# A state space mixer whose output projection runs three groups behind instead of two, with the last group's steps placed between its shares

## The chip, the cores and the metric

The kernel runs on one core of a Trainium2 chip. The metric is the device time of one launch in microseconds; the runs shown are medians over repeated launches. TensorE (PE) is granted one of two clock levels, 2.4 GHz (shown as 1.00) or 1.2 GHz (0.50).

## The reference

A decoder trunk of two layers on 256 tokens of width 1024, in float32. Each layer is a half SwiGLU block, a token mixer, and another half SwiGLU block. The first layer's mixer is a Mamba-2 state space mixer with 8 groups of 4 heads of 64 channels and a state of 128; the second's is latent attention. The change touches the first mixer only, which is:

```
def mamba2_mixer(h, w_in, conv_w, conv_b, dt_bias, a_log, d_skip, norm_w, w_out):
    proj = h @ w_in
    z, xbc, dt = ...                       # 2048, 2048 + 2*1024, 32 columns
    xbc = silu(causal_depthwise_conv(xbc, conv_w, conv_b))
    xs, bm, cm = ...                       # 8 groups x 4 heads x 64; 8 x 128; 8 x 128
    y = ssd_chunked(xs, dt, a, bm, cm)     # chunks of 128 tokens
    y = y + d_skip * xs
    g = (y * silu(z)) in 8 groups of 256
    g = g * rsqrt(mean(g*g, within the group) + EPS) * norm_w
    return g @ w_out                       # 2048 -> 1024
```

## The kernel before, in words

**Matrix products.** Every float32 product is made of three matmuls on rounded parts (`mm3`, L203 to L205): high weight by high activation, high weight by low activation, low weight by high activation. A weight tile arrives by DMA on SP's queue (`raw`, four buffers, 128x1024, which is 8 matrices of 128x128 and so 24 matmuls of the mixer). ACT casts it to the high part (`whi`, L119), DVE subtracts to get the low part (`wlo`, L121); five pairs of `whi`/`wlo` can be held. The tiles come in one fixed order, that in which the host packed them (`packed_weights`), and `ws.next()` hands them out in the same order, so a step that is moved takes its weights with it.

**The mixer.** For each group g of 8 there are these steps:

- `stage_x`: 16 `mm3` (48 matmuls) into an accumulator, then a convolution: DVE scales into `up` (L383), ACT makes two products, POOL adds them (L398), DVE adds two more taps for two tiles (L401), ACT applies SiLU.
- `stage_z`: 48 matmuls, scaled on DVE (L645), SiLU on ACT.
- `stage_bc(g + 2)`: 48 matmuls and a convolution for B and C, two groups ahead.
- `stage_a`, for two groups at once in every even g: C by B on PE (L509, L510), copied by ACT to `cbm`; a DMA from SP brings `acb` (L516, two buffers); DVE adds masks (L522, L525), ACT takes exponentials (L531, L534) and DVE multiplies into `dec` (L538).
- `stage_t`: four transposes of xs (L552), scaled by DVE to `xd` (L557).
- `stage_y`: eight matmuls of `dec` by `xd` (L571, L574), DVE adds the skip term (L581, `y`), POOL multiplies by z (L586, `gt`) and squares and adds (L239, L242, L243, `gsq`).
- `stage_n`: a sum over the channels on PE (L249), DVE scales it (L253, `rsv`), POOL takes the power -1/2 (L257, `rsc`).
- `stage_o`: PE spreads `rsc` (L264), DVE multiplies (L601, `gn`), ACT and DVE split the result into `yh` (L228) and `yl` (L229).
- `stage_out(g)`, the share of the group in the output: 48 matmuls, six into each half of four accumulators that are kept until the mixer's end, when x is added (L626).

PSUM has four `acc` and four `misc` buffers. Projections use `acc` until the first share takes all four for the output, from then on `misc`. Every engine runs its instructions in one fixed order. That order is made by a scheduler when the program is built: it starts from the order in which the code is written, and moves instructions past one another within the limits of buffers and data.

Of the kernel before, what the change touches and what calls it, by code (L numbers as in the profile page):

```python
# [10 lines left out]
F32 = mybir.dt.float32  # L11
# [8 lines left out]
P = 128  # L20
# [3 lines left out]
KD = D // P  # L24
# [5 lines left out]
NG = 8  # L30
# [134 lines left out]
def trunk(ctx: ExitStack, tc: tile.TileContext, xt, pos, wts, small, consts, out):  # L165
# [201 lines left out]
    def ssm(n, nxt):  # L367
        with tc.tile_pool(name="mp", bufs=2) as mp:
# [134 lines left out]
            def stage_a(g):  # L503

                bc = st.pop((g, "bc"))
                ps = misc_ps()
                nc.tensor.matmul(ps[:, :T], bc[:, 0, :P], bc[:, 1], start=True, stop=True)  # L509
                nc.tensor.matmul(  # L510
                    ps[:, T : T + P], bc[:, 0, P:], bc[:, 1, P:], start=True, stop=True
                )
                cb = mp.tile([P, 3 * P], F32, tag="cbm", name="cbm")
                nc.scalar.copy(cb, ps[:, : 3 * P])
                acb = mp.tile([P, 4, T], F32, tag="acb", name="acb")
                nc.sync.dma_start(  # L516
                    acb, acd[4 * g : 4 * g + 4].unsqueeze(0).broadcast_to([P, 4, T])
                )

                mask = cst[:, C_TM : C_TM + P].unsqueeze(1).broadcast_to([P, 4, P])  # L520
                acm = mp.tile([P, 4, P], F32, tag="acm", name="acm")
                nc.vector.tensor_tensor(  # L522
                    out=acb[:, :, :P], in0=acb[:, :, :P], in1=mask, op=ALU.add
                )
                nc.vector.tensor_tensor(out=acm, in0=acb[:, :, P:], in1=mask, op=ALU.add)  # L525
                ms = []
                for hp in range(2):
                    dec = mp.tile([P, 2, 3 * P], F32, tag="dec", name="dec", bufs=8)
                    for j in range(2):
                        h = 4 * g + 2 * hp + j  # L530
                        in_turn(nc.scalar.activation(  # L531
                            dec[:, j, :T], acb[:, 2 * hp + j], AF.Exp, bias=bias[:, h : h + 1]
                        ))
                        in_turn(nc.scalar.activation(  # L534
                            dec[:, j, T:], acm[:, 2 * hp + j], AF.Exp,
                            bias=bias[:, NH + h : NH + h + 1],
                        ))
                    nc.vector.tensor_tensor(  # L538
                        out=dec, in0=dec,
                        in1=cb.unsqueeze(1).broadcast_to([P, 2, 3 * P]),  # L540
                        op=ALU.mult,
                    )
                    ms.append(dec)
                st[g, "m"] = ms

            def stage_t(g):

                xs = st[g, "x"]
                ps = misc_ps()
                for b in range(NB):  # L550
                    for j in range(2):
                        nc.tensor.transpose(  # L552
                            ps[:, (2 * b + j) * P : (2 * b + j + 1) * P],
                            xs[:, j, b * P : (b + 1) * P], ident,
                        )
                xd = mp.tile([P, NB, 4, HD], F32, tag="xd", name="xd")
                nc.vector.tensor_tensor(  # L557
                    out=xd, in0=ps.rearrange("p (b h c) -> p b h c", b=NB, h=4),
                    in1=dt.rearrange("p (b h) -> p b h", b=NB)[:, :, 4 * g : 4 * g + 4]
                    .unsqueeze(3).broadcast_to([P, NB, 4, HD]),  # L560
                    op=ALU.mult,
                )
                st[g, "xd"] = xd
# [28 lines left out]
            def stage_n(g):  # L592
                st[g, "r"] = rs_col(st.pop((g, "q")), 2 * P)
# [13 lines left out]
                two_part(yh, yl, gn)  # L607
                st[g, "y"] = yh, yl

            def stage_out(g, half):  # L610

                yh, yl = st[g, "y"]
                if not outs:
                    outs.extend(acc_ps() for _ in range(KD // 2))
                for d in range(4 * half, 4 * half + 4):
                    o = outs[d // 2][:, d % 2 * T : (d % 2 + 1) * T]
                    for k in range(2):

                        mm3(
                            o, ws.next(), yh[:, k], yl[:, k],  # L620
                            g == 0 and d % 2 == 0 and k == 0,
                            g == NG - 1 and d % 2 == 1 and k == 1,
                        )
                    if g == NG - 1 and d % 2 == 1:
                        both = x[:, d - 1 : d + 1]
                        nc.vector.tensor_tensor(  # L626
                            out=both, in0=both, in1=wide(outs[d // 2]), op=ALU.add
                        )
                        use_x(nxt, d - 1)
                        use_x(nxt, d)  # L630
# [21 lines left out]
            for g in range(NG):  # L652
                stage_x(g)
                if g == 0:
                    bias, acd = sums()
                else:
                    stage_y(g - 1)
                stage_z(g)
                if g:
                    stage_n(g - 1)  # L660
                stage_t(g)
                if g % 2 == 0:
                    stage_a(g)
                    stage_a(g + 1)
                if g:
                    stage_o(g - 1)
                if g + 2 < NG:
                    stage_bc(g + 2)
                if g == last:
                    stage_y(last)  # L670
                if g > 1:
                    stage_out(g - 2, 0)
                    stage_out(g - 2, 1)
            stage_n(last)
            stage_out(last - 1, 0)
            stage_o(last)
            stage_out(last - 1, 1)
            stage_out(last, 0)
            stage_out(last, 1)

    def angles():

# [369 lines left out]
def packed_weights(a):  # L1052

    seq = []

    def add(ts):
        seq.append(np.ascontiguousarray(ts.reshape(-1, P, P)))

    def ffn(i, j):
        g, u = tiles_of(a["ffn_w_gate"][i, j]), tiles_of(a["ffn_w_up"][i, j])  # L1060
        gu = np.stack([g, u])
        add(gu[:, :, :2].transpose(1, 2, 0, 3, 4))
        add(gu[:, :, 2:].transpose(2, 1, 0, 3, 4))
        add(tiles_of(a["ffn_w_down"][i, j]).transpose(1, 0, 2, 3))

    def by_column(w):
        add(tiles_of(w).transpose(1, 0, 2, 3))

    def by_pair(w0, w1):
        add(np.stack([tiles_of(w0)[:, 0], tiles_of(w1)[:, 0]], 1))  # L1070

    def narrow(w):

        w = w.reshape(KD, P, NARROW).transpose(1, 0, 2).reshape(P, KD * NARROW)
        add(w.reshape(P, -1, P).transpose(1, 0, 2))

    ffn(0, 0)
    w = a["ssm_w_in"][0]
    wz, wx, wb, wc, wd = np.split(w, [DI, 2 * DI, 2 * DI + 1024, 2 * DI + 2048], axis=1)
    narrow(wd)  # L1080

    def bc(g):
        by_column(wb[:, P * g : P * g + P])
        by_column(wc[:, P * g : P * g + P])

    def out(g):
        by_column(a["ssm_w_out"][0][256 * g : 256 * g + 256])

    bc(0)
    bc(1)  # L1090
    for g in range(NG):
        by_column(wx[:, 256 * g : 256 * g + 256])
        by_column(wz[:, 256 * g : 256 * g + 256])
        if g + 2 < NG:
            bc(g + 2)
        if g > 1:
            out(g - 2)
    out(NG - 2)
    out(NG - 1)
    ffn(0, 1)  # L1100
    ffn(1, 0)
    w = a["mla_w_in"][0]
    wq, wkv, wr = np.split(w, [QL, QL + KVL], axis=1)
    by_pair(wq[:, :P], wq[:, P : 2 * P])
    by_column(wq[:, 2 * P :])
    by_column(wkv)
    narrow(wr)
    kv = a["mla_w_kv_b"][0].reshape(KVL, MH, NOPE + VD)
    wk, wv = (
        tiles_of(np.ascontiguousarray(part).reshape(KVL, MH * 64))  # L1110
        for part in (kv[:, :, :NOPE], kv[:, :, NOPE:])
    )
    wq = tiles_of(a["mla_w_q_b"][0])
    for i in range(2):
        for t, n, c in ((wq, 3, 2 * i), (wq, 3, 2 * i + 1), (wk, 4, i), (wv, 4, i)):
            add(t[:, n * c : n * c + n])
    by_column(a["mla_w_out"][0][:512])
    by_column(a["mla_w_out"][0][512:])
    ffn(1, 1)

    tiles = np.concatenate(seq)
    out = np.empty(tiles.size, tiles.dtype)
    n0 = 0
    for n in SIZES:
        out[n0 * P * P : (n0 + n) * P * P] = (
            tiles[n0 : n0 + n].transpose(1, 0, 2).reshape(-1)
        )
        n0 += n
    assert n0 == len(tiles)
    return out  # L1130
# [63 lines left out]
```

## Time and profile before

| | |
|---|---|
| median of the runs | 1134.09 us (1133.56 to 1136.16, 3 runs) |
| the profiled execution | 1136.57 us, its span 1134.5 us |
| mean granted clock | 0.982 |
| PE busy | 1092.2 us (96% of the span) |
| DVE busy | 852.1 us (75%) |
| ACT busy | 642.8 us (57%) |
| POOL busy | 211.5 us (19%) |

The span is the part of the profiled execution between its first and last instruction. An engine's share is its busy time over the span; a PE at half clock counts as busy too.

### The profile page before, as it was taken

The page shows a single profiled execution, that of the slowest core. Times are in us where ns is not written, and L with a number is a line of the kernel's source. Part 1 is how long each engine was busy: PE and PEld are TensorE (multiplying, and loading weights), DVE is VectorE, ACT ScalarE, POOL GpSimd, SP SyncE. Part 2 cuts the span into 40 slices and gives each one's busy share as a digit, 9 for nine tenths or more (in the row PEclk, how much of TensorE's full clock was granted, in tenths as well). Part 3 has the DMA queues.
Part 4 walks back from the last instruction along what each step waited for, and adds up shares of the span by engine and source line. Part 5 has one row for each costly group of instructions (what it writes and reads, how often), then busy time and mean ns, then how long its engine had stood idle before and what let it go on. Part 6 is the DMA issues. An engine that isn't in the chain of part 4 may idle for free.

```text
span 1134.5 us, 18325 instructions
## 1 busy us (share of the span) xinstructions
PE 1092.2 (96%) x6902; PEld 974.0 (86%) x6902; DVE 852.1 (75%) x1370; ACT 642.8 (57%) x1102; POOL 211.5 (19%) x201
## 2 busy tenths in 40 slices
PE   7999999998999988999999999999996999999998
PEld 6888888997998987888888988888995689888887
DVE  7877776789777876877777687776779768877653
ACT  5655544677657564555554475554465545655541
POOL 7000012204223224200002200001247025000000
PEclk9999999998989998999999999999998999999999
DMA  7766665565345442655555575555543025665661
GB/s 240 226 185 187 187 187 171 181 201 175 133 146 168 158 133 97 200 187 189 189 186 168 186 236 191 185 186 187 168 148 117 1 64 170 204 186 186 187 204 55
DMA packets 55320, 191.58 MB, mean 169 GB/s; under 512 B 6304, under 2 KB 8384, under 8 KB 55232
## 3 DMA queue, kind: packets, MB, share of 16 engines
q1 hardware_dynamic: 55200, 190.41, 52.5%
q8 instruction: 54, 0.88, 0.3%
q14 instruction: 34, 0.28, 0.1%
q0 software_dynamic: 32, 0.00, 0.0%
HBM read 189.31 MB, written 1.08 MB: 168 GB/s over the span
## 4 chain that ended last, share of the span: by engine, by line
PE 80%; DVE 11%; DMA 3%; ACT 2%; issue 2%; POOL 2%; SPq 0%; DVEq 0%; ACTq 0%
PE acc L214 40%; PE misc L214 21%; PE acc L203 3%; PE acc L204 3%; PE acc L205 3%; DVE wlo L121 3%; PE misc L203 2%; DVE ca L401 2%; PE misc L204 2%; PE misc L205 2%; DMA acb<-acd 1%; PE acc L983 1%; POOL xsq L243 1%; DMA cst<-consts 1%; DVE qc L892 1%
## 5 line engine op out<-in xcount | busy, mean ns | idle before, releaser
L121 DVE TENSOR_TENSOR wlo<-raw,whi 128x1024 fp32r<-128x1024 f32 (+3 forms) x345 | 433.6, 1260 | 158.4 <-ACT whi L119 157.3
L119 ACT CAST whi<-raw 128x1024 fp32r<-128x1024 f32 (+3 forms) x355 | 364.8, 1031 | 251.9 <-PE acc L214 139.6
L214 PE MATMUL misc<-xp,whi 128*128 128x512 f32 x704 | 279.8, 401 | 0.4 <-ACT whi L119 0.4
L214 PE MATMUL acc<-xp,whi 128*128 128x512 f32 x704 | 274.8, 393 | 0.0
L214 PE MATMUL acc<-ap,whi 128*128 128x512 f32 x616 | 215.5, 397 | 0.0
L214 PE MATMUL misc<-xp,wlo 128*128 128x256 f32 x704 | 196.5, 281 | 3.5 <-DVE wlo L121 3.5
L214 PE MATMUL acc<-xp,wlo 128*128 128x256 f32 x704 | 197.1, 282 | 0.2 <-DVE wlo L121 0.2
L214 PE MATMUL acc<-ap,wlo 128*128 128x256 f32 x616 | 167.8, 281 | 0.0
L214 PEld LDWEIGHTS acc<-xp,whi 128*128 128x128 f32 x704 | 132.2, 188 | 33.1
L214 PEld LDWEIGHTS misc<-xp,whi 128*128 128x128 f32 x704 | 132.4, 189 | 23.2 <-ACT whi L119 0.7
L214 PEld LDWEIGHTS misc<-xp,wlo 128*128 128x128 f32 x704 | 132.7, 189 | 11.4 <-DVE wlo L121 4.2
L214 PEld LDWEIGHTS acc<-ap,whi 128*128 128x128 f32 x616 | 113.9, 188 | 25.5
L214 PEld LDWEIGHTS acc<-xp,wlo 128*128 128x128 f32 x704 | 133.0, 189 | 1.3 <-DVE wlo L121 0.5
L214 PEld LDWEIGHTS acc<-ap,wlo 128*128 128x128 f32 x616 | 115.4, 188 | 2.8
L320 ACT COPY g<-misc 128x256 f32<-128x256 f32 x88 | 32.7, 371 | 82.2 <-PE misc L214 82.0
L239 POOL TENSOR_TENSOR xsq<-x 128x256 f32<-128x256 f32 x6 | 3.7, 612 | 366.0 <-DVE x L364 351.5
L242 POOL TENSOR_TENSOR sq<-x 128x256 f32<-128x256 f32 x42 | 40.2, 963 | 115.3 <-DVE x L364 112.2
L205 PE MATMUL acc<-xp,wlo 128*128 128x256 f32 x216 | 61.6, 285 | 0.0
L204 PE MATMUL acc<-xp,whi 128*128 128x256 f32 x216 | 61.6, 285 | 0.0
L203 PE MATMUL acc<-xp,whi 128*128 128x256 f32 x216 | 61.4, 286 | 0.0
L203 PE MATMUL misc<-xp,whi 128*128 128x256 f32 x208 | 60.6, 291 | 0.0
L204 PE MATMUL misc<-xp,whi 128*128 128x256 f32 x208 | 59.5, 286 | 0.0
(249 smaller groups left out, 1926.4 us busy)
## 6 DMA issues: line engine op xcount, KB each, us to landing
raw<-wts SPq DMA_DIRECT2D x341, 512.0 KB, 4.0
acb<-acd SPq DMA_DIRECT2D x8, 512.0 KB, 3.7
raw<-wts SPq DMA_DIRECT2D x8, 256.0 KB, 2.8
raw<-wts SPq DMA_DIRECT2D x4, 384.0 KB, 3.0
out<-x SPq DMA_DIRECT2D x8, 128.0 KB, 3.3
x<-xt SPq DMA_DIRECT2D x3, 256.0 KB, 7.1
raw<-wts SPq DMA_DIRECT2D x4, 192.0 KB, 2.3
sm<-small SPq DMA_DIRECT2D x1, 283.5 KB, 7.9
```

Of the source, the lines that this page charges most:

```text
L119: self.nc.scalar.copy(hi[:, :n], raw[:, :n])
L121: eng.tensor_tensor(out=lo[:, :n], in0=raw[:, :n], in1=hi[:, :n].bitcast(F32), op=ALU.subtract)
L203: nc.tensor.matmul(o, w[0], h, start=start, stop=False)
L204: nc.tensor.matmul(o, w[0], l, start=False, stop=False)
L205: nc.tensor.matmul(o, w[1], h, start=False, stop=stop)
L214: nc.tensor.matmul(dst, a, b, start=start and i == 0, stop=stop and i == 1)
L242: nc.gpsimd.tensor_tensor(out=sq, in0=src, in1=src, op=ALU.mult)
L243: nc.gpsimd.tensor_tensor(out=acc, in0=acc, in1=sq, op=ALU.add)
L320: nc.scalar.copy(t, ps[:, T:])
L401: nc.vector.scalar_tensor_tensor(out=a[:, j], in0=up[:, j, k : k + T], scalar=w(t, k), in1=a[:, j], op0=ALU.mult, op1=ALU.add,)
L892: eng.tensor_tensor(out=a, in0=a, in1=r[:, b, o].unsqueeze(2).broadcast_to(list(a.shape)), op=ALU.mult,)
L983: nc.tensor.matmul(o, vt[:, 0, c], pT[:, :T], start=True, stop=False)
```

## The change

The share of a group in the output comes three groups behind the projections instead of two, and the host packs the output's tiles in that order. Within an iteration the steps of earlier groups change their places: `stage_o` comes right behind `stage_x` and for the group before last, `stage_y` behind `stage_z`, `stage_n` behind `stage_bc`, `stage_t` behind all of these. After the loop, the last group's transposes, products and norm are written between the last three shares, which are cut by output columns. `dec` has six buffers instead of eight.

```diff
-                    dec = mp.tile([P, 2, 3 * P], F32, tag="dec", name="dec", bufs=8)
+                    dec = mp.tile([P, 2, 3 * P], F32, tag="dec", name="dec", bufs=6)
...
-            def stage_out(g, half):
+            def stage_out(g, d0=0, d1=KD):
...
-                for d in range(4 * half, 4 * half + 4):
+                for d in range(d0, d1):
...
                 stage_x(g)
                 if g == 0:
                     bias, acd = sums()
-                else:
-                    stage_y(g - 1)
+                if g > 1:
+                    stage_o(g - 2)
                 stage_z(g)
                 if g:
-                    stage_n(g - 1)
-                stage_t(g)
+                    stage_y(g - 1)
                 if g % 2 == 0:
                     stage_a(g)
                     stage_a(g + 1)
-                if g:
-                    stage_o(g - 1)
                 if g + 2 < NG:
                     stage_bc(g + 2)
-                if g == last:
-                    stage_y(last)
-                if g > 1:
-                    stage_out(g - 2, 0)
-                    stage_out(g - 2, 1)
+                if g:
+                    stage_n(g - 1)
+                if g < last:
+                    stage_t(g)
+                if g > 2:
+                    stage_out(g - 3)
+
+            stage_t(last)
+            stage_o(last - 1)
+            stage_out(last - 2, 0, 4)
+            stage_y(last)
+            stage_out(last - 2, 4, 8)
+            stage_out(last - 1, 0, 4)
             stage_n(last)
-            stage_out(last - 1, 0)
+            stage_out(last - 1, 4, 6)
             stage_o(last)
-            stage_out(last - 1, 1)
-            stage_out(last, 0)
-            stage_out(last, 1)
+            stage_out(last - 1, 6, 8)
+            stage_out(last)
...
-        if g > 1:
-            out(g - 2)
-    out(NG - 2)
-    out(NG - 1)
+        if g > 2:
+            out(g - 3)
+    for g in range(NG - 3, NG):
+        out(g)
```

The scheduler settles what this does to each engine. **PE at the first share, before:** the spread of group 0 (L264), the products of group 1, and then at once the first matmuls of group 0's share (`yh_2737`, `yl_2738`), which take the accumulators `acc_3118` to `acc_3121`.

```order
L264 MATMUL misc_2731<-cst_73,rsc_2722 128x128 x2
L571 MATMUL misc_2891<-dec_2471,xd_2729 64x256
L574 MATMUL misc_2891<-dec_2471,xd_2729 64x128
...
L571 MATMUL misc_2891<-dec_2477,xd_2729 64x256
L574 MATMUL misc_2891<-dec_2477,xd_2729 64x128
L203 MATMUL acc_3118<-yh_2737,whi_2943 128x256
L203 MATMUL acc_3119<-yh_2737,whi_2943 128x256
...
L204 MATMUL acc_3118<-yl_2738,whi_2943 128x256
L205 MATMUL acc_3118<-yh_2737,wlo_2944 128x256
```

**The same place after:** behind the spread (`rsc_2797`) and group 1's products come four matmuls of `stage_a` and a projection (`xp` is the mixer's input).

```order
L264 MATMUL misc_2881<-cst_73,rsc_2797 128x128 x2
L571 MATMUL misc_2956<-dec_2464,xd_2804 64x256
...
L574 MATMUL misc_2956<-dec_2470,xd_2804 64x128
L509 MATMUL misc_2975<-bc_2537 128x256
L510 MATMUL misc_2975<-bc_2537 128x128
L509 MATMUL misc_2997<-bc_2778 128x256
L510 MATMUL misc_2997<-bc_2778 128x128
L203 MATMUL acc_3108<-xp_75,whi_2924 128x256
```

The first share (`yh_2887`) now starts 164 matmuls later in PE's order than before and fills its accumulators one after the other (`acc_3366` to `acc_3369`). Before its last accumulator stands the norm's sum of group 2:

```order
L205 MATMUL acc_3368<-yh_2887,wlo_3281 128x256
L249 MATMUL misc_3352<-ones_76,gsq_3272 128x1 x2
L203 MATMUL acc_3369<-yh_2887,whi_3280 128x256
L204 MATMUL acc_3369<-yl_2888,whi_3280 128x256
```

**DVE in the stretch ahead of the first shares, before:** the scaling of group 1's norm (`rsv_2978`) stands behind one mask pair and ahead of the `dec` of groups 2 and 3.

```order
L522 TENSOR_TENSOR acb_3678<-acb_3678,cst_73 128x4x128
L525 TENSOR_TENSOR acm_3680<-acb_3678,cst_73 128x512
L253 TENSOR_SCALAR rsv_2978<-misc_2975 128x2
L557 TENSOR_TENSOR xd_2987<-misc_2982,dt_2199 128x512
L121 TENSOR_TENSOR wlo_3186<-raw_3152,whi_3185 128x1024
L538 TENSOR_TENSOR dec_2999<-dec_2999,cbm_2992 128x768
```

**After:** group 1's scaling (`rsv_3097`) stands behind three of the four `dec` of groups 2 and 3 and the mask pair `acb_3604`. Later on DVE, from the second weight tile of the first share (`wlo_3227`) on, ten entries stand up to the reading of `acc_3277`, whose PSUM the share's last accumulator takes over.

```order
L538 TENSOR_TENSOR dec_2985<-dec_2985,cbm_2978 128x768
L538 TENSOR_TENSOR dec_2991<-dec_2991,cbm_2978 128x768
L383 TENSOR_TENSOR up0_2055<-acc_3108,rs_2123 128x2x256
L538 TENSOR_TENSOR dec_3007<-dec_3007,cbm_3000 128x768
L522 TENSOR_TENSOR acb_3604<-acb_3604,cst_73 128x4x128
L525 TENSOR_TENSOR acm_3606<-acb_3604,cst_73 128x512
L253 TENSOR_SCALAR rsv_3097<-misc_3094 128x2
```

```order
L121 TENSOR_TENSOR wlo_3227<-raw_3194,whi_3226 128x1024
L601 SCALAR_TENSOR_TENSOR gn_3186<-gt_2968,sm_72,misc_3183 128x256 x2
L645 TENSOR_TENSOR zt_3254<-acc_3193,rs_2123 128x512
L121 TENSOR_TENSOR wlo_3281<-raw_3224,whi_3280 128x1024
L401 SCALAR_TENSOR_TENSOR ca_3171<-up0_2055,sm_72,ca_3171 128x256 x2
L581 SCALAR_TENSOR_TENSOR y_3267<-xs_2867,sm_72,misc_3258 128x256 x2
L121 TENSOR_TENSOR wlo_3311<-raw_3278,whi_3310 128x1024
L229 TENSOR_TENSOR yl_3190<-gn_3186,yh_3189 128x512
L121 TENSOR_TENSOR wlo_3373<-raw_3308,whi_3372 128x1024
L401 SCALAR_TENSOR_TENSOR ca_3171<-up0_2055,sm_72,ca_3171 128x256 x2
L383 TENSOR_TENSOR up1_2056<-acc_3277,rs_2123 128x2x256
```

**DVE at the mixer's end, before:** the low part of group 6 (`yl_4647`) stands ahead of group 7's skip term.

```order
L557 TENSOR_TENSOR xd_4638<-misc_4633,dt_2199 128x512
L601 SCALAR_TENSOR_TENSOR gn_4643<-gt_4554,sm_72,misc_4640 128x256 x2
L229 TENSOR_TENSOR yl_4647<-gn_4643,yh_4646 128x512
L581 SCALAR_TENSOR_TENSOR y_4659<-xs_4528,sm_72,misc_4650 128x256 x2
L121 TENSOR_TENSOR wlo_4809<-raw_4776,whi_4808 128x512
```

**After,** a weight tile and group 7's skip term stand ahead of it.

```order
L557 TENSOR_TENSOR xd_4638<-misc_4633,dt_2199 128x512
L601 SCALAR_TENSOR_TENSOR gn_4643<-gt_4559,sm_72,misc_4640 128x256 x2
L121 TENSOR_TENSOR wlo_4769<-raw_4729,whi_4768 128x512
L581 SCALAR_TENSOR_TENSOR y_4689<-xs_4458,sm_72,misc_4680 128x256 x2
L229 TENSOR_TENSOR yl_4647<-gn_4643,yh_4646 128x512
```

On PE the order from the spread of group 6 to the mixer's end is the same in both programs. On SP the DMAs of `acb` keep their places among themselves, and the weight loads between those of groups 2 and 3 and those of groups 4 and 5 fall from 14 to 12.

## Rows read from the trace of the kernel before

**Rows 1.** The profile's page: its span, and one group of its fifth part.

```profile
span 1134.5 us, 18325 instructions
...
L121 DVE TENSOR_TENSOR wlo<-raw,whi 128x1024 fp32r<-128x1024 f32 (+3 forms) x345 | 433.6, 1260 | 158.4 <-ACT whi L119 157.3
```

**Rows 2.** PE's timeline: start, duration, line, operation, tiles, and [idle before, releaser].

```profile
267.58 0.27 PE L249 MATMUL misc<-ones,gsq 128*128 128x1 f32 x1 [1.37 <-POOL gsq L243]
...
274.65 0.38 PE L264 MATMUL misc<-cst,rsc 128*128 128x128 f32 x2
...
280.01 0.58 PE L203 MATMUL acc<-yh,whi 128*128 128x256 f32 x1 [3.45 <-ACT yh L228]
...
314.08 0.48 PE L264 MATMUL misc<-cst,rsc 128*128 128x128 f32 x1 [2.19 <-POOL rsc L257]
...
369.12 0.38 PE L205 MATMUL acc<-yh,wlo 128*128 128x256 f32 x1 [2.91 <-DVE wlo L121]
...
421.83 0.27 PE L249 MATMUL misc<-ones,gsq 128*128 128x1 f32 x1 [1.03 <-POOL gsq L243]
...
425.65 0.47 PE L552 MATMUL misc<-cst,xs 128*128 128x128 f32 x1 [3.21 <-ACT xs L405]
...
437.13 0.32 PE L264 MATMUL misc<-cst,rsc 128*128 128x128 f32 x1 [1.03 <-POOL rsc L257]
439.50 0.58 PE L203 MATMUL acc<-yh,whi 128*128 128x256 f32 x1 [1.94 <-ACT yh L228]
```

**Rows 3.** Windows: us, then PE, PEld, DVE, ACT, POOL busy (count); clock, DMA, GB/s.

```profile
212.00:232.00 20.00, 20.00 (x170) 19.80 (x169) 18.79 (x34) 17.40 (x27) 4.01 (x3) 1.00 0.53 168
268.64:272.03 3.39, 3.39 (x18) 3.39 (x17) 3.39 (x5) 0.09 (x1) 1.10 (x1) 0.50 0.75 259
280.01:285.69 5.68, 5.67 (x24) 5.28 (x25) 5.14 (x7) 4.88 (x11) 4.70 (x5) 0.50 0.29 95
314.08:319.82 5.74, 5.74 (x27) 5.74 (x28) 2.61 (x4) 0.72 (x2) 0.00 (x0) 0.50 0.53 181
371.02:374.43 3.41, 3.17 (x15) 2.48 (x14) 2.68 (x6) 1.96 (x3) 0.70 (x1) 0.50 0.62 226
425.65:429.05 3.40, 3.04 (x16) 2.27 (x18) 1.57 (x4) 1.08 (x2) 0.00 (x0) 0.50 0.55 194
439.50:442.70 3.20, 3.20 (x15) 3.20 (x16) 0.67 (x1) 0.00 (x0) 0.00 (x0) 0.50 0.33 122
```

**Rows 4.** POOL's timeline: group 0's power, and group 7's product by z.

```profile
273.63 0.87 POOL L257 TENSOR_TENSOR rsc<-rsv,mhalf 128x2 f32<-128x2 f32 x1 [3.89 <-DVE rsv L253]
...
415.06 1.30 POOL L586 TENSOR_TENSOR gt<-y,zs 128x512 f32<-128x512 f32 x1 [16.45 <-ACT cb L397]
```

**Rows 5.** DVE's mask pair of `stage_a`, and SP's waits for ACT (total, times, longest).

```profile
289.05 0.69 DVE L522 TENSOR_TENSOR acb<-acb,cst 128x512 f32<-128x512 f32 x1 [3.90 <-DMA acb<-acd]
...
SPq L516 <- ACT dec L534: 16.0, 5, 5.8
```

**Rows 6.** DVE and PE at the start of group 6's share.

```profile
428.95 0.69 DVE L229 TENSOR_TENSOR yl<-gn,yh 128x512 fp32r<-128x512 f32 x1 [0.69 <-ACT yh L228]
429.85 0.87 DVE L581 SCALAR_TENSOR_TENSOR y<-xs,sm,misc 128x256 f32<-128x256 f32 x2 [0.21 <-PE misc L574]
...
430.32 0.28 PE L204 MATMUL acc<-yl,whi 128*128 128x256 f32 x1
```

**Rows 7.** Two windows, and DVE's convolution pairs with POOL busy and idle.

```profile
240.00:320.00 80.00, 71.92 (x544) 68.73 (x542) 66.10 (x90) 51.92 (x91) 23.42 (x20) 0.89 0.51 169
302.91:308.78 5.87, 5.87 (x52) 5.87 (x51) 5.42 (x7) 1.91 (x2) 5.71 (x5) 1.00 0.69 238
...
305.21 2.27 DVE L401 SCALAR_TENSOR_TENSOR ca<-up,sm,ca 128x256 f32<-128x256 f32 x2
308.01 1.45 DVE L401 SCALAR_TENSOR_TENSOR ca<-up,sm,ca 128x256 f32<-128x256 f32 x2
327.91 0.87 DVE L401 SCALAR_TENSOR_TENSOR ca<-up,sm,ca 128x256 f32<-128x256 f32 x2
```

## The prediction

> **What bounds the kernel now.** I read the page first: PE is busy for 96% of the span. So I ask only where PE stands still and where it runs at half clock, and I ask it of the mixer, about 199 to 447 us of the span, since PE's order differs nowhere else. Two views answer this.
>
> PE's timeline gives the idle time ahead of each matmul and what ended it. Eight waits of a microsecond or more stand in the mixer [rows 2]. Three are in the front, up to the first shares: 1.37 us at 267.58 for the squares of group 0, 3.45 at 280.01 for the high part of group 0, at the very first matmul of the first share, and 2.19 at 314.08 for a norm. That is 7.0 us. One is in the middle, 2.91 at 369.12. Two are in the tail, 1.03 at 421.83 and 3.21 at 425.65, where group 7's transposes wait for SiLU: 4.2 us. Two end the stage, 1.03 and 1.94: 3.0 us. The sum is 17.1 us.
>
> The windows give the granted clock. At full clock 170 matmuls take 20.00 us, 0.118 us each [rows 3]. Six stretches behind such waits were granted 0.50, the 1.2 GHz level [rows 3]. Half of PE's busy time there is lost: 1.7, 2.8 and 2.9 us in the front (7.4), 1.6 in the middle, 1.5 in the tail, 1.6 at the end, together 12.1 us. The wait at 421.83 was followed by no such stretch, those at 267.58 and 437.13 to 439.50 were.
>
> So the mixer holds 29.2 us that other orders could win, 14.4 of it in the front. Nothing in the change removes a matmul: what it gives is waits and the clock behind them.
>
> **The change part by part.**
>
> *The first share comes 164 matmuls later.* Before, PE went from the spread of group 0 through group 1's eight products straight into the share, and the chain behind the spread (gn on DVE, the cast on ACT, yl on DVE) had only those products as its cover. Now 164 matmuls by 0.118 us, 19 us, lie between. The 3.45 us go, and so does the half clock behind them. The wait at 314.08 is one of the old order too: there the spread came eight instructions behind the norm's sum; now it stands 33 to 62 behind it in the first three groups, 3.9 us or more, where eight by 0.118 and the 2.19 of the wait, 3.1 us, would have done.
>
> *What waits in the front instead.* Five places, each from the new order with the old durations.
> - Sum of group 0: DVE reaches group 0's y behind the same instructions as before, so the squares are ready at the same time, and PE has four matmuls more ahead of the sum: 1.37 - 4 x 0.118 = 0.9 us.
> - Spread of group 0: before it started at 274.65 with no wait [rows 2], 7.07 us behind the sum, of which 1.7 were half clock. At full clock with eight matmuls more it would come after 6.3 us, at 273.9. The power ended at 274.50 [rows 4], and two convolution taps more stand ahead of it on DVE, some 0.8 us (a pair takes 0.87 [rows 7]), so 275.2: a wait of 1.3. If the clock falls behind the sum as before, PE comes 1.7 later and waits for nothing; the two exclude each other.
> - Spread of group 1: its scaling now stands on DVE behind the mask pair, and that behind the DMA of acb, for which DVE waited 3.90 us [rows 5]. Up to 3 us can come through, or nothing where DVE is behind anyway. I take 1.2.
> - Sum of group 2 and the share's fourth accumulator go together. From the share's second weight tile on, DVE has ten entries up to the last reading of that PSUM: three weight tiles at 1.26 [rows 1], two convolution pairs, gn and y at 0.87, three of 0.69 like yl [rows 6], together 9.3 us. PE has 36 share matmuls there, 4.25 us. If DVE leads by two weight tiles, 2.5 us, 2.5 are left, by three, 1.3; with no lead it is 5.1, with four tiles in hand nothing. I take 1.9, between two and three of the five pairs.
>
> Together 5.3 us in the front for 7.0. For the clock I take two stretches like the first, 1.7 us each, since these waits lie about the 1.03 at 421.83 that cost no clock and the 1.37 at 267.58 that did: 3.4 for 7.4, with bounds of nothing and 7.4.
>
> *The middle.* The wait at 369.12 was for a low part that stood late on DVE in a share. In the new order spread, norm sum and share of one group lie an iteration apart, and in groups 3 to 6 I find no consumer nearer to its producer than before. I take 0.5 for 4.5 (2.91 + 1.6), with both as bounds.
>
> *The tail.* Group 7's transposes have 124 matmuls between x's projection and themselves, where there were 104: 20 x 0.118 = 2.4 us. On POOL the convolution's sum now stands ahead of the 1.30 us product by z [rows 4], not behind it. Together 3.7 us against 3.21, so this wait and its half clock go, and the 1.03 ahead of it, for squares that POOL made late, goes with the sum's place. New: yl of group 6 stands behind y of group 7 on DVE. Before, it ended at 429.64, and the matmul that reads it started at 430.32 [rows 6]. Behind y, which ended at 430.72, it ends at about 431.3: a wait of 1.0 us. Tail: 1.0 for 5.8.
>
> *The end.* From the spread of group 6 on PE's order is the same, and 4.6 us (3.0 and 1.6) stay.
>
> *Edits that cost nothing.* Six dec buffers: a pair of groups makes four, and the products of the group before have freed two by then; if they hadn't, DVE would wait about the 0.95 us of a product once in each even group. The packing moves no byte more. ACT and DVE do the same work as before.
>
> *The sum.* After: 5.3 + 3.4 + 0.5 + 1.0 + 4.6 = 14.8 us for 29.2. The gain is 14.4 us against the profiled execution's own 1136.57 us, whose span is 1134.5 [rows 1]: 1122.2. That execution lies 2.5 us above the median of the runs, so the median comes out at 1119.7, which I round to 1120. The front at nothing gives 1111; the front at its old 14.4 (7.0 and 7.4) and the middle at its old 4.5 give 1130.
>
> **The rivals.**
>
> *DVE becomes the bound of the front (1125 to 1131.8).* For 80 us in the front DVE is busy for 66.1 and POOL for 23.4 [rows 7]. With no share to do, PE takes a projection's weights at 2.8 us a tile while DVE still owes y, gn, masks and dec; if each microsecond of POOL's came on top of DVE's work, 89.5 us would have to fit into 80, and 9.5 us come back: 1129 (from 5 on I count it here). For it: with POOL busy, convolution pairs took 2.27 and 1.45 us instead of 0.87 [rows 7]. Against it: in that stretch of 5.71 us of POOL work this is 2.0 us more on DVE, about a third, already counted in the 66.1. The Trainium skill ("SBUF — State Buffer", section "Who interferes with whom") calls the port pair that DVE and GpSimd share an exclusive lock, and says that a DVE instruction with two SBUF inputs contends with a GpSimd instruction that reads SBUF. By that rule in its hardest form the sum would be this rival's 1129; the trace shows a part of it, 2.0 of 5.71 us.
>
> *The small waits don't come and the clock stays up (1109 to 1115).* Where DVE's lead is larger than I took it, the front's 8.7 us shrink to 1 or so: 1119.7 - 7.7 = 1112. For it: of the waits that I forecast in the front none is over 1.9 us. Against it: 1.37 us at 267.58 was enough for half clock.
>
> *Waits only move (within 0.2%).* The chain of a group is as long as it was and DVE is busy throughout the front, so each wait removed can return at the next thing that PE needs from DVE. Front, middle and tail would keep their 24.6 us: 1134. Against it: the largest waits were at places where the order gave a chain no cover, and DVE had idle time elsewhere.
>
> *SP's queue starves PE (slower, about 1142).* The DMA of acb waits on SP for ACT's exponentials, 16.0 us in five times, up to 5.8 [rows 5], and every weight load behind it waits as well. Of the loads between the pairs, 14 became 12, so the DMA comes two loads, 48 matmuls, earlier on SP, and could wait longer there. If the three pairs each cost PE 5.8 us and a half clock of 1.6, that is 3 x 7.4 = 22.2 us against the 14.4 won: 1134.1 + 7.8 = 1142. It decides only where SP's wait exceeds the four loaded tiles in hand, 4 x 24 x 0.118 = 11.3 us; the longest was 5.8.
>
> **How the numbers follow.** The forecast, 1115 to 1125, has 0.45; DVE as the bound 0.22; the quiet case 0.15; waits that only move 0.09; SP's queue 0.09. 0.2%, 2.3 us, is about what a measurement of this kernel can tell from no change. The first three are faster by more than that, 0.82; same 0.09; slower 0.09. The range of 1109 to 1133 leaves out SP's queue and the upper half of the case without change.
>
> **What the changed kernel's profile would show.** Right: no wait of over 1 us ahead of the first share's L203, none at L552 of group 7, waits of 0.9 to 1.9 us at L249 and L264 of groups 0 to 2 and at the share's fourth accumulator, one at the L204 of group 6's share, the same two at the end, and three stretches of half clock at most where there were six. PE's busy time in the mixer falls by the clock, its idle time by the waits. Wrong: DVE busy without a gap in the front while PE waits for wlo (the first rival), an L89 wait on SP with raw as PE's or ACT's releaser behind the acb DMAs (the last), or new waits in groups 3 to 6, which I took to be free of them.

## The result and the profile after

The changed kernel takes 1120.11 us (median of 4 runs, 1119.69 to 1121.53) against 1134.07 us: 14.0 us less. The ratio is 0.9882, its 95% interval 0.9865 to 0.9899. The profiled execution took 1121.53 us.

The page's span, PE's timeline and four windows of the changed kernel answer [rows 1 to 3].

```profile
span 1119.4 us, 18325 instructions
```

```profile
265.04 0.38 PE L249 MATMUL misc<-ones,gsq 128*128 128x1 f32 x2 [0.80 <-POOL gsq L243]
...
273.86 0.38 PE L264 MATMUL misc<-cst,rsc 128*128 128x128 f32 x1 [2.15 <-POOL rsc L257]
...
304.98 0.37 PE L249 MATMUL misc<-ones,gsq 128*128 128x1 f32 x1 [3.32 <-POOL gsq L243]
...
361.99 0.27 PE L249 MATMUL misc<-ones,gsq 128*128 128x1 f32 x1 [1.26 <-POOL gsq L243]
...
415.00 0.39 PE L204 MATMUL acc<-yl,whi 128*128 128x256 f32 x1 [0.65 <-DVE yl L229]
...
421.91 0.32 PE L264 MATMUL misc<-cst,rsc 128*128 128x128 f32 x1 [1.03 <-POOL rsc L257]
...
424.29 0.58 PE L203 MATMUL acc<-yh,whi 128*128 128x256 f32 x1 [1.95 <-ACT yh L228]
```

```profile
240.00:320.00 80.00, 73.52 (x579) 70.09 (x579) 69.64 (x95) 55.57 (x96) 27.98 (x22) 0.94 0.51 171
273.99:277.41 3.42, 3.42 (x19) 2.12 (x19) 3.42 (x6) 2.73 (x5) 0.00 (x0) 0.50 0.65 205
304.71:311.54 6.83, 6.57 (x30) 6.57 (x31) 3.34 (x5) 1.97 (x4) 2.16 (x3) 0.50 0.49 154
424.18:427.59 3.41, 3.30 (x15) 3.30 (x16) 0.69 (x1) 0.06 (x1) 0.00 (x0) 0.50 0.36 132
```

The reader is to see that the wait of 3.45 us at the first share is gone, and group 7's transposes no longer wait (3.21 before). In the front other waits stand in their place: 2.15 us at the spread of group 0 and 3.32 at the sum of group 2. Of six stretches at 1.2 GHz three are left, one of them 6.83 us long. The two waits at the end are what they were.

**The mixer in four numbers.** From the start of the last matmul ahead of the mixer to that of the first behind it, the timeline has 191.79 to 446.76 us before, 255.0 us (the first two rows), and after (the last two):

```profile
191.79 0.40 PE L214 MATMUL acc<-ap,whi 128*128 128x512 f32 x1
...
446.76 0.40 PE L214 MATMUL misc<-xp,whi 128*128 128x512 f32 x1
```

```profile
189.46 0.40 PE L214 MATMUL acc<-ap,whi 128*128 128x512 f32 x1
...
431.59 0.40 PE L214 MATMUL misc<-xp,whi 128*128 128x512 f32 x1
```

That is 242.1 us, 12.8 less. Taking off PE's waits in the mixer (all of 0.08 us or more) and half of PE's busy time at half clock leaves nearly the same in every kernel of this study, so these two terms hold the whole effect. Stretches are counted from the mixer's start: the front is the first 130 us, the middle the next 83, the end the rest. Each entry is waits + loss by the clock, in us.

| kernel | mixer | front | middle | end | left |
|---|---|---|---|---|---|
| before | 255.0 | 8.1 + 7.4 | 3.1 + 1.6 | 7.6 + 3.1 | 224.1 |
| changed | 242.1 | 6.5 + 5.0 | 1.5 + 0 | 3.8 + 1.7 | 223.7 |

The front gave 4.0 us, the middle 3.2, the end 5.2. The profiled executions differ by 15.0 us (1136.57 to 1121.53). 2.3 us of that lie ahead of the mixer (191.79 to 189.46), where PE's order is the same in both: the execution of before was granted half clock from 12.62 to 16.03 us, that of after full clock there.

```profile
12.62:16.03 3.41, 3.18 (x10) 2.80 (x11) 3.41 (x5) 2.76 (x4) 3.41 (x4) 0.50 1.03 402
```

```profile
12.62:16.03 3.41, 3.31 (x19) 2.65 (x18) 3.41 (x5) 1.96 (x4) 3.33 (x4) 1.00 1.01 397
```

The first row is of before, the second of after: 10 matmuls for 19 in the same time. So the profile credits the change with 12.8 us, the medians with 14.0. The 1.2 us between them can't be placed, since only one execution of each was profiled.

### The profile page after: what moved, and what is told of

The parts are those of the page before. It is cut to its first block, busy times and chain, and to the rows that moved or that the text cites. A ratio compares the mean times of both kernels' runs of the same rounds, so it can differ in the third digit from the quotient of the medians.

```text
span 1119.4 us, 18325 instructions
## 1 busy us (share of the span) xinstructions
PE 1083.5 (97%) x6902; PEld 967.1 (86%) x6902; DVE 846.4 (76%) x1370; ACT 642.2 (57%) x1102; POOL 216.9 (19%) x201
## 4 chain that ended last, share of the span: by engine, by line
PE 57%; DVE 4%; POOL 1%; ACT 1%; issue 0%; ACTq 0%; DVEq 0%
PE acc L214 31%; PE misc L214 16%; PE acc L203 2%; PE acc L204 2%; PE acc L205 2%; PE acc L987 1%; POOL xsq L243 1%; DVE qc L896 1%; POOL sq L242 1%; PE misc L949 1%; PE misc L909 1%; PE misc L974 0%; PE misc L947 0%; PE acc L988 0%; DVE ro L833 0%; ACT whi L119 0%
## 5 line engine op out<-in xcount | busy, mean ns | idle before, releaser
L214 PE MATMUL acc<-xp,wlo 128*128 128x256 f32 x704 | 197.1, 282 | 0.5 <-DVE wlo L121 0.3
L204 PE MATMUL acc<-xp,whi 128*128 128x256 f32 x264 | 74.6, 283 | 0.0
L203 PE MATMUL acc<-xp,whi 128*128 128x256 f32 x264 | 74.4, 283 | 0.0
L205 PE MATMUL acc<-xp,wlo 128*128 128x256 f32 x264 | 74.2, 281 | 0.0
L243 POOL TENSOR_TENSOR xsq<-xsq,sq 128x256 f32<-128x256 f32 x45 | 51.7, 1149 | 2.6
L321 DVE TENSOR_TENSOR g<-misc,g 128x256 f32<-128x256 f32 x88 | 37.1, 422 | 18.2 <-ACT g L320 18.2
```

Of the source, the lines that this page charges most:

```text
L203: nc.tensor.matmul(o, w[0], h, start=start, stop=False)
L204: nc.tensor.matmul(o, w[0], l, start=False, stop=False)
L205: nc.tensor.matmul(o, w[1], h, start=False, stop=stop)
L214: nc.tensor.matmul(dst, a, b, start=start and i == 0, stop=stop and i == 1)
L243: nc.gpsimd.tensor_tensor(out=acc, in0=acc, in1=sq, op=ALU.add)
L321: nc.vector.tensor_tensor(out=t, in0=ps[:, :T], in1=t, op=ALU.add)
```

## The experiments

Theory: the gain is waits and the clock behind them, and the distance of the share from its spread carries the front. Rivals: the steps' new places do it all; DVE bounds the front; POOL's chain does, stretched by DVE. Each kernel ran beside the kernel before on the same chip. The tail needed no run: with the tail written as in the kernel before (or the new tail in the kernel before), the scheduler gives all five engines the same order. With eight `dec` buffers in the changed kernel the orders of PE, DVE and ACT are the same too.

### Which part of the change does it

**Shares two groups behind, steps in the new places (steps_lag2).**

```diff
-                if g > 2:
-                    stage_out(g - 3)
+                if 1 < g < last:
+                    stage_out(g - 2)
```

The host's packing follows in this run as in the others that move shares.

> The steps in their new places, but the shares only two groups behind (packed in that order). In this order the first share stands right behind the spread, group 1's products and four matmuls of stage_a, as in the kernel before. Theory (the distance of the first share and the distance between sum and spread each give their part): the wait ahead of the first share comes back, about 3 us, with a half-clock stretch of 2.8, the rest stays won: about 1126. Rival one (the new places of the steps do it all, the third group is not needed): 1120. Rival two (the third group does it all): 1134.

1120.27 us, ratio 0.9878 (0.9865 to 0.9891): the same as the whole change. Rival one has it. PE's timeline of this kernel in the front:

```profile
267.77 0.27 PE L249 MATMUL misc<-ones,gsq 128*128 128x1 f32 x1 [2.61 <-POOL gsq L243]
...
274.18 0.32 PE L264 MATMUL misc<-cst,rsc 128*128 128x128 f32 x1 [1.17 <-POOL rsc L257]
...
279.02 0.39 PE L203 MATMUL acc<-yh,whi 128*128 128x256 f32 x1 [1.40 <-ACT yh L228]
...
280.73 0.39 PE L204 MATMUL acc<-yl,whi 128*128 128x256 f32 x1 [0.98 <-DVE yl L229]
```

With the first share behind the spread and group 1's products, as before, PE waits 2.4 us there instead of 3.45, and 6.2 us in the front in all; with the share 164 matmuls later it waits 6.5. Between these two kernels the waits moved, they didn't shrink. No half clock followed them in this execution.

**Shares three behind, steps in the old places (lag3_old_steps).** The loop of the kernel before with `stage_out(g - 3, ...)`, and the share of group 5 behind the loop.

> The shares three groups behind and packed so, with the steps where they were in the kernel before. The first share is far from its spread, but the spread of group 2 stands directly behind the norm's sum. Theory: no wait ahead of the first share, about 3 us of waiting and 2.9 us of half clock at a spread in the front, and some of the middle's 4.5: about 1127. Rival one (the steps do it all): 1134. Rival two (the third group does it all): 1120.

1131.14 us, 0.9979 (0.9968 to 0.9990). So the distance of the share alone is worth about 3 us, less than the theory's 7. In the front the share now waits for something else, the PSUM of an accumulator that DVE still reads:

```profile
302.42 0.35 PE L203 MATMUL acc<-yh,whi 128*128 128x256 f32 x1 [3.29 <-DVE up L383]
```

**One step alone: stage_o later (o_only).**

```diff
+                if g > 1:
+                    stage_o(g - 2)
                 stage_z(g)
...
-                if g:
-                    stage_o(g - 1)
+                if g == last:
+                    stage_o(last - 1)
```

> The kernel before with one step moved: stage_o stands an iteration later, for the group before last. In this order the spread is 96 or more matmuls behind the sum from group 1 on, and the first share stands right behind the spread of group 0. If the distance from sum to spread is what matters, the wait of 2.19 us at the spread with its half clock (2.9), the middle's wait and most of the tail go: 1122 to 1125. If the places of y, n and t matter, 1129 to 1134.

1135.41 us, 1.0015 (1.0007 to 1.0024): nothing won. The wait at the spread went, but three shares now wait over a microsecond for the low or high part (3.94 us at 279.03, 1.48 at 332.85, 3.73 at 364.80), and products wait 1.73 us for `xd` and 2.11 for `dec`. The first share stands right behind its spread. The other two stand a projection (48 matmuls) behind theirs, and there the low part comes late on DVE: ahead of it a weight tile took 2.32 us, where 1.21 is usual, and a convolution pair 1.58 instead of 0.87 (last rows).

```profile
279.03 0.38 PE L203 MATMUL acc<-yh,whi 128*128 128x256 f32 x1 [3.94 <-ACT yh L228]
...
364.80 0.58 PE L204 MATMUL acc<-yl,whi 128*128 128x256 f32 x1 [3.73 <-DVE yl L229]
```

```profile
359.79 2.32 DVE L121 TENSOR_TENSOR wlo<-raw,whi 128x1024 fp32r<-128x1024 f32 x1
362.03 1.58 DVE L401 SCALAR_TENSOR_TENSOR ca<-up,sm,ca 128x256 f32<-128x256 f32 x2
363.54 1.21 DVE L229 TENSOR_TENSOR yl<-gn,yh 128x512 fp32r<-128x512 f32 x1
```

**Transposes alone (t_only).** `stage_t(g)` moved from ahead of `stage_a` to behind `stage_bc`.

> The kernel before with one step moved: the transposes (stage_t) stand behind stage_bc, one projection later; o, y and n as before, shares two groups behind. o alone measured 1135.4, y, n and o without t 1129.2, all four 1120.3. If t's late place gives its own 9 us, 1125; if it works only together with the others (in this order the spread stands 16 or fewer matmuls behind the sum, or directly behind it), 1130 to 1136.

1136.48 us, 1.0030 (1.0019 to 1.0042): 0.3% slower. Spreads close behind their sum wait 2.06 to 2.21 us in three groups, and the products wait for the transposes' result (2.88 us at 277.78).

```profile
277.78 0.44 PE L571 MATMUL misc<-dec,xd 128*64 128x256 f32 x2 [2.88 <-DVE xd L557]
...
372.33 0.32 PE L264 MATMUL misc<-cst,rsc 128*128 128x128 f32 x1 [2.21 <-POOL rsc L257]
```

**Products, sums and spreads late, transposes early (y_n_o_late).** In each iteration x, o, z, y, t, a, bc, n, share; shares two behind.

> The kernel before with y, n and o in their new places, and only the transposes (stage_t) where they were, shares two groups behind. steps_lag2, which moves the transposes too, measured 1120.3. If the transposes' place is worth nothing, 1120; if group 7's transposes without cover (3.21 us and 1.5 of half clock before) are bound to their place, 1123 to 1125.

1129.15 us, 0.9952 (0.9938 to 0.9967): 4.8 of the 13.8 us. Its mixer is 10.0 us longer than that of steps_lag2: 5.1 us more of waits, 4.7 more of half clock. The waits that steps_lag2 hasn't got stand at the transposes, which wait for SiLU four times (3.7 us), and at two spreads (2.90 at 350.36, 1.89 at 417.11):

```profile
258.08 0.33 PE L552 MATMUL misc<-cst,xs 128*128 128x128 f32 x1 [1.01 <-ACT xs L405]
...
308.13 0.33 PE L552 MATMUL misc<-cst,xs 128*128 128x128 f32 x1 [1.00 <-ACT xs L405]
...
350.36 0.32 PE L264 MATMUL misc<-cst,rsc 128*128 128x128 f32 x1 [2.90 <-DVE up L383]
...
414.23 0.33 PE L552 MATMUL misc<-cst,xs 128*128 128x128 f32 x1 [1.37 <-ACT xs L405]
```

In steps_lag2 no transpose waits, and the spreads wait 1.17 and 0.53 us, besides the last, which waits 1.03 in both. So the transposes' place is worth about 9 us with the other three steps moved and nothing alone; o alone and t alone only move the stall to the next step of the same chain. Other sets, such as t and o without y and n, were not run: that all four are needed is not shown.

### What sets the front

**The product by z on DVE (gt_on_dve).** `nc.vector.tensor_tensor` for `nc.gpsimd.tensor_tensor` at L586. The reason is a row of the changed kernel: POOL took 3.95 us for group 2's product, 1.29 for group 0's.

```profile
258.73 1.29 POOL L586 TENSOR_TENSOR gt<-y,zs 128x512 f32<-128x512 f32 x1 [18.36 <-DVE y L581]
...
297.62 3.95 POOL L586 TENSOR_TENSOR gt<-y,zs 128x512 f32<-128x512 f32 x1 [3.00 <-DVE y L581]
```

> The changed kernel with the product of y by z (L586, eight of them) on DVE instead of POOL. In the changed kernel PE waits 3.32 us at 304.98 for the squares of group 2, whose product took POOL 3.95 us beside DVE's work. Theory (POOL's product, stretched by DVE's instructions on the same data, makes the chain late): that wait falls below 1 us and its half clock of 6.83 us goes, DVE pays 0.7 us eight times: 1114 to 1117. Rival (DVE is the bound of the front, busy without a gap from 265 to 305 us): the wait stays or moves to wlo, 1121 to 1124.

1121.32 us, 0.9895 (0.9883 to 0.9908): as the changed kernel, at best; the theory missed, the time is the rival's. But the order changed with the edit: the scheduler put the product on DVE behind five entries that follow y, at 304.46, and a convolution's addition (2.24 us at 307.28) between the squares on POOL. The sum of group 2 waited longer, the front's waits came to 9.1 us, and what the stretched product costs stays untested:

```profile
310.25 0.37 PE L249 MATMUL misc<-ones,gsq 128*128 128x1 f32 x1 [5.10 <-POOL gsq L243]
```

**The squares on ACT (squares_on_act).**

```diff
-                for j in range(2):
-                    add_square(sq, gt[:, j], j == 0)
+                s2 = sp.tile([P, T], F32, tag="sq", name="sq")
+                nc.scalar.activation(sq, gt[:, 0], AF.Square)
+                nc.scalar.activation(s2, gt[:, 1], AF.Square)
+                nc.gpsimd.tensor_tensor(out=sq, in0=sq, in1=s2, op=ALU.add)
```

> The changed kernel with the two squares of a group (L239, L242) on ACT, the product by z and the addition still on POOL. Theory of POOL's chain: the product stays stretched, only about 1.4 us of squares leave POOL's chain for 1.2 us on ACT, so the wait of 3.32 us shrinks little, to 2 or 3 us: 1118 to 1120. Rival (POOL's total time beside DVE is what counts): each microsecond taken off POOL gives DVE its time back, 1115 to 1117. Rival two (ACT's casts come late): 1122 or more.

1126.53 us, 0.9938 (0.9926 to 0.9951): slower than the changed kernel, by rival two, though not by casts. POOL had the product ready at 385.45, but the squares stood on ACT behind the exponentials of two groups and a cast until 391.36, and PE waited 5.04 us (the front's waits came to 8.0 us):

```profile
393.36 0.37 PE L249 MATMUL misc<-ones,gsq 128*128 128x1 f32 x1 [5.04 <-POOL gsq L591]
```

**Less work on DVE (less_dve_front).** The last of four taps is left out in four convolutions, so the output isn't the reference's.

```diff
-                for k in (2, 3):
+                for k in (2,) if 6 <= count[0] <= 9 else (2, 3):
```

> The changed kernel with the last tap of four convolutions left out (x of groups 2 and 3, B and C of 3 and 4), so that DVE has eight instructions of 0.4 us, 3.2 us in all, less to do in the front; PE's order there moves by a few matmuls only. In the kernels so far PE waits some 6 us in the front in any order of the shares, and DVE is busy without a gap from 265 to 305 us. If DVE bounds the front, the waits there fall from 6.3 to 3 or 4 us, and perhaps the half clock behind the longest (up to 3.4): 1113 to 1117. If the chains' latency sets the waits, 1119 to 1120.

1120.84 us, 0.9882 (0.9869 to 0.9895): no change. The front's waits are 6.1 us, the sum of group 2 still waits 2.81. That speaks against DVE's amount of work as the bound. A row says why the time isn't given on: POOL's addition took 4.06 us beside two weight tiles on DVE, and DVE then stood still 1.19 us for it.

```profile
291.84 4.06 POOL L398 TENSOR_TENSOR ca<-ca,cb 128x512 f32<-128x512 f32 x1 [1.51 <-ACT cb L397]
...
295.94 0.48 DVE L401 SCALAR_TENSOR_TENSOR ca<-up,sm,ca 128x256 f32<-128x256 f32 x1 [1.19 <-POOL ca L398]
```

**The second tap on DVE, no addition on POOL (front_add_on_dve, front_add_steps_lag2).** In four convolutions of the front:

```diff
+                front = 5 <= count[0] <= 8
                 count[0] += 1
...
-                nc.gpsimd.tensor_tensor(out=a, in0=a, in1=b, op=ALU.add)
-                for k in (2, 3):
+                if not front:
+                    nc.gpsimd.tensor_tensor(out=a, in0=a, in1=b, op=ALU.add)
+                for k in (1, 2, 3) if front else (2, 3):
```

> The changed kernel where, in four convolutions of the front (the same as in less_dve_front), DVE adds the second tap itself (eight instructions of 0.4 us more, 3.2 us), in place of ACT's second product and POOL's addition (L398), which took 1.3 to 4.1 us each beside DVE. Opposite in sign to less_dve_front, which took 3.2 us from DVE and left the waits at 6.1. If POOL and DVE holding one another up is what sets the front, the waits fall below 4 us and the half clock of 5.1 shrinks: 1114 to 1118. If DVE's work sets it, 3 us more: 1122 to 1125. If the order's distances set it, 1120.

> The same four additions on DVE, on the order with shares two groups behind (steps_lag2, 1120.3, front waits of 6.2 us and no half clock there). POOL theory: 1115 to 1118; DVE's work: 1122 to 1125; distances: 1120.

1120.33 us (0.9882, 0.9869 to 0.9895) and 1119.88 us (0.9880, 0.9867 to 0.9892): each as its kernel without the edit. The sum of group 2 waits only 0.75 us in the first, but the share's accumulator then waits 3.46 us for the read that I had forecast:

```profile
303.40 0.51 PE L203 MATMUL acc<-yh,whi 128*128 128x256 f32 x1 [3.46 <-DVE up L384]
```

The waits of the front come to 6.7 and 5.3 us. In the seven kernels with the four steps in their new places and the product and squares on POOL they are 5.3 to 6.7, whether work is taken from DVE, POOL's additions are given to DVE, or the share is moved; with the product or the squares off POOL they are 9.1 and 8.0.

### The end, and a version that beats both

**Group 7's products ahead of the shares (early_last_y).** Written as t, y, share 4, o, n, share 5, o, shares 6 and 7.

> The changed kernel with the last group's products written ahead of the shares of groups 4 and 5, not between them. The scheduler then puts group 7's products ahead of group 6's spread, and 14 matmuls between the last sum and the last spread where there were none. If the last 4.6 us (1.03 and 1.94 of waiting and 1.6 of half clock) are made by that lack of cover, 14 x 0.118 = 1.7 us take the first wait away and perhaps the clock's part: 1116 to 1118. If the wait only moves, 1120.

1122.99 us, 0.9902 (0.9890 to 0.9915): a miss, longer than either case, though its interval overlaps that of the change. The end's waits are 4.1 us for 3.8: the 1.03 at the last spread went, and a wait of 2.04 at group 6's share came.

```profile
415.82 0.38 PE L203 MATMUL acc<-yh,whi 128*128 128x256 f32 x1 [2.04 <-ACT yh L228]
...
425.93 0.39 PE L203 MATMUL acc<-yh,whi 128*128 128x256 f32 x1 [1.69 <-ACT yh L228]
```

**Shares four groups behind (lag4).** `stage_out(g - 4)`, one more share behind the loop, four buffers of `yh` and `yl`.

> The changed kernel with the shares four groups behind (four yh and yl buffers, packed so). A further 48 matmuls are left for the end: 20 of them stand between group 6's spread and group 7's products, 5 between the last sum and the last spread. If distance of the shares pays at the end, the wait at group 6's low part (0.65) goes and the 1.03 at the last spread halves: 1118 to 1119. The front has one iteration more without a share: if that is dear there, 1122 to 1125.

1115.19 us (5 runs, 1113.82 to 1117.88), 0.9839 (0.9827 to 0.9852): faster than both kernels (its interval and that of the change, 0.9865 to 0.9899, don't meet), by more than I expected. Its timeline, the stretch that the changed kernel ran at half clock, here at full clock, and the one stretch at half clock in its mixer:

```profile
273.75 0.32 PE L264 MATMUL misc<-cst,rsc 128*128 128x128 f32 x1 [2.17 <-POOL rsc L257]
...
289.87 0.32 PE L264 MATMUL misc<-cst,rsc 128*128 128x128 f32 x1 [1.43 <-POOL rsc L257]
...
304.85 0.27 PE L249 MATMUL misc<-ones,gsq 128*128 128x1 f32 x1 [1.86 <-POOL gsq L243]
...
416.17 0.32 PE L264 MATMUL misc<-cst,rsc 128*128 128x128 f32 x1 [0.34 <-POOL rsc L257]
...
418.29 0.38 PE L203 MATMUL acc<-yh,whi 128*128 128x256 f32 x1 [1.69 <-ACT yh L228]
```

```profile
273.99:277.41 3.42, 3.42 (x30) 2.85 (x29) 3.42 (x5) 2.83 (x5) 0.00 (x0) 1.00 0.65 229
...
419.99:423.41 3.42, 3.42 (x19) 3.42 (x18) 0.69 (x1) 0.91 (x2) 1.00 (x2) 0.50 0.37 143
```

| kernel | mixer | front | middle | end | left |
|---|---|---|---|---|---|
| changed | 242.1 | 6.5 + 5.0 | 1.5 + 0 | 3.8 + 1.7 | 223.7 |
| steps_lag2 | 240.2 | 6.2 + 0 | 1.3 + 0 | 5.1 + 3.2 | 224.5 |
| lag3_old_steps | 250.6 | 8.2 + 6.8 | 4.8 + 0 | 3.8 + 1.7 | 225.3 |
| o_only | 255.9 | 8.8 + 3.1 | 5.4 + 3.4 | 7.2 + 3.4 | 224.8 |
| t_only | 255.9 | 9.6 + 5.0 | 5.1 + 0 | 7.3 + 4.0 | 225.0 |
| y_n_o_late | 250.2 | 7.7 + 0 | 2.9 + 1.7 | 7.0 + 6.2 | 224.6 |
| lag4 | 236.1 | 5.7 + 0 | 2.1 + 0 | 2.4 + 1.7 | 224.2 |

Of lag4's 6.1 us over the changed kernel, 1.4 are waits at the end, 5.0 the front's half clock, which did not come; the rest nearly cancels. Not all of the 5.0 can be put down to the order. PE, DVE, ACT and POOL run the same order in both programs up to the first share, at 297 us, so the 1.7 us behind the wait at 273.8 differ between two executions of the same order. And early_last_y, whose order in the front is the changed kernel's on every engine, lost 3.4 us there, not 5.0. Nor is lag4's lead the clock alone: its five executions had a mean granted clock of 0.987 to 0.992 over the span, and the one at 0.987 took 1115.19 us, while the changed kernel's shortest took 1119.69 at 0.991. How the lead divides between order and clock, one profile of each doesn't show.

## Why the prediction was right, and where its steps were not

The forecast was 1120 us and the median is 1120.11, but the sum behind it came out at 14.8 us of waits and clock left in the mixer, and the profile shows 18.5.

- **Front, waits: 5.3 forecast, 6.5 measured, against 8.1 before.** The sum of group 0 was right (0.9; 0.80). The spread of group 0 was taken too small (1.3; 2.15), the spread of group 1 too large (1.2; none). The sum of group 2 and the fourth accumulator were taken at 1.9 together; 3.32 came, all at the sum: by its rows POOL's product took 3.95 us ahead of it, where I had counted DVE's entries alone.
- **Front, clock: 3.4 forecast, 5.0 measured.** Two stretches came, one twice as long as I took.
- **The step that failed** is "The first share comes 164 matmuls later": I let 19 us of cover carry the largest term of the gain. The wait at the share did go, but steps_lag2, with the share where it was, takes the same time and has the same waits in the front. There the rival of waits that only move held: 8.1 us became 6.5. What the front gained in these profiles is mostly clock (7.4 to 5.0), and nothing ties this term to the share: it was 0 in steps_lag2 and lag4 at waits of 6.2 and 5.7, and 3.4 in early_last_y with the changed kernel's own order.
- **Middle: 0.5 forecast, 1.5 measured, against 4.7.** Right in kind. The 1.26 us at a sum is a wait in groups 3 to 6, which I took to be free of them and whose waits I had named as a sign of being wrong.
- **Tail: 1.0 forecast, 0.8 measured.** The transposes' wait went and the low part of group 6 waits 0.65 us behind group 7's y. This term was right. The hand-cut tail has no part in it.
- **End: 4.6, as forecast** (1.03, 1.95 and 1.7 of clock). early_last_y shows that it moves when the order is changed without more work to cover it; lag4 lowers it to 4.1.
- **Size of the gain:** 14.4 forecast, 12.8 in the mixer's profile, 14.0 by the medians. Of what is left after I had 3.7 us too little; of what was there before I had left out 1.7 us of small waits, and the rest of the mixer came out 0.4 us shorter: 14.4 - 3.7 + 1.7 + 0.4 = 12.8. With the 1.2 us that can't be placed this is the 14.0 of the medians. So part of the closeness is luck: misses that cancelled.
- **The rivals.** SP's queue starving PE: SP's wait for ACT grew from 16.0 us to 17.8 in six times, the longest 6.1, and no wait of PE in the mixer has a weight part as its releaser. DVE as the bound: it was busy for 39.99 of the 40 us from 265 to 305, but PE waited there for no weight part, and less_dve_front speaks against its amount of work. DVE and POOL holding one another up is seen in rows (3.95 and 4.06 us for 1.3), and the Trainium skill ("SBUF — State Buffer", section "Who interferes with whom") tells of it as an exclusive lock on the port pair that the two engines share. These rows agree. But taking four additions off POOL won nothing, so that it costs the kernel time is not shown.

**What stays open:** what holds the front's waits at 5 to 7 us once the four steps are in their new places, and why half clock came behind them in some executions and not in others.

## What to carry to other kernels

A chain of small steps (square, sum, power, spread, split, use) in a stream of matmuls needs cover, that is other matmuls to run meanwhile, at every link: here moving one link gave its wait to the next, and moving four steps won 13.8 us with no change in the work. Count waits and half-clock time by stage in each profile; if what is left is the same, the two terms are the whole effect, and a right total can be checked term by term. And profile more than one execution before crediting an order with clock: the same order of the front lost 5.0 us in one and 3.4 in another.

## What the runs showed of the hardware that was not expected

- The clock does not follow the length of a wait alone. Behind 2.15 us at 273.86 the changed kernel was granted 0.50, with 19 matmuls in the next 3.42 us; behind 2.17 us at 273.75, in the same place of the program and with the same order of PE, DVE, ACT and POOL up to there, lag4 was granted 1.00, with 30 matmuls. Over the whole front the loss was 5.0 us in the one execution and nothing in the other, beside waits of 6.5 and 5.7.
- POOL's product of 128x512 took 1.29 to 3.95 us in the changed kernel and an addition 4.06 us in less_dve_front, with DVE at work beside them; where the product took 1.29 us at 258.73, the weight tile beside it on DVE took 1.98 us instead of 1.21. A convolution pair on DVE took 2.27 us in place of 0.87 with POOL busy [rows 7].
